# Spreading the retention work over projection slots, using weight slabs one by one over eight PSUM banks, threading transposes between matmuls, and reordering the first loads

## The chip, the cores and the metric

The kernel runs on one Trainium2 chip, as the same program on all 8 cores (two dies, cores 0 to 3 and 4 to 7); each core computes one batch element. The time is the device time of the slowest core in microseconds (us).

In most executions the runs agree within 0.3%; in some, the cores of one die or both show a lower granted TensorE clock and the run is longer. All comparisons below use fast runs. Even in fast runs, some *pairs* of cores (0 and 1, 2 and 3, ...) show a stretch of about 150 us at a clock of 0.81, which costs such a pair some 30 us. I therefore compare stages on a core without such a stretch.

Engine names as the profile has them: PE is TensorE (matmul), DVE is VectorE, ACT is ScalarE, POOL is GpSimd, SP is SyncE (here the issuer of the small DMAs; the big weight slabs are issued from POOL's queue).

## The reference, cut to what matters

One transformer-like layer over 2048 tokens of width 2048, plus 256 context tokens:

```python
h  = modulate(rmsnorm(x, norm1_g), sh1, sc1)        # shift, scale, gate from silu(c) @ w_mod
p  = h @ w_in                                       # q, k, v, g_ret, u, vs, two merge gates
ret = bidirectional_retention(rope(q), rope(k), v, lg_f, lg_b, s_f, s_b)  # 8 heads of 256
ret = per_head_rmsnorm(ret) * silu(g_ret)
y_sg = spatial_gating(gelu(u), gelu(vs), ...)       # layernorm(vs), 128x128 mixing of positions
x  = x + gt1 * ((sig(gr) * (ret @ w_ret_o) + sig(gs) * (y_sg @ w_sg_o)) @ w_out)
h2 = modulate(rmsnorm(x, norm2_g), sh2, sc2)
x  = x + gt2 * ((silu(a) * b) @ w_ffn_out)          # a, b = split(h2 @ w_ffn_in), width 5632
return rmsnorm(x, final_norm_g)
```

The kernel goes through it in this order: modulation columns (`wm` slabs); head by head keys and values (`wk`, `wv`), then queries and output gates (`wq`, `wg`) with the retention itself in between; then for each half of the tokens the gate values (`wvs`), the gate inputs (`wu`), the two merged branches (`wgr`, `wgs`), the output projection (`wo`), and the FFN in and out (`wfi`, `wfo`, twice, since the hidden width is split in two).

## The kernel before

All work is issued by a small framework that records reads and writes and adds semaphore waits. Each engine runs its instructions in program order. Weights come through a stream of four slab buffers: `WS.next` takes the next loaded slab, `WS.done` gives its buffer to the next load. The parts that matter here:

```python
# start: everything small first, then the weight stream
dist = ...; F.dma("sp", dist[:], distd); ...; F.dma("sp", wsf[:], sgw...)
WS.pump()
load_x(xkeys[:6])
... # decay tables of all heads on VectorE and ScalarE, each stored to DRAM (two buffers)
... # wsT: transposes of the small mixing weights
norm_x(0, xkeys[0:4])                       # norm of token block 0: ScalarE squares, VectorE rest
for s in range(16):
    mod_cols(s, bank(s % 4))                # 32 tiny matmuls, VectorE adds the bias and frees the bank
    if s == 11:
        F.wait("sp", WS.tickets[12]); load_x(xkeys[6:10])
# ...
# retention pieces are threaded between projections: a "slot" is one projection unit
RV = Rr([2, 3]); RO = Rr([4, 5]); RA = Rr([6, 7])          # rings of PSUM banks
def q_unit(ib, wq):
    ...
    for dst, tt_ in ((qf, tf), (qb, tb)):                    # decayed queries, both on POOL
        F.tt("pool", dst, q, tt_, ALU.mult)
    at(n + 2, lambda: scores(2 * ib + 1)); at(n + 2, lambda: scores(2 * ib))
    at(n + 3, lambda: outp(2 * ib + 1));   at(n + 4, lambda: outp(2 * ib))
for ib in (3, 2, 1, 0):
    at(n, lambda ib=ib: b_step(2 * ib + 1)); at(n + 2, lambda ib=ib: b_step(2 * ib))
    at(n + 3, lambda ib=ib: mod_cols(16 + 4 * h + 3 - ib, bank(RA.get())))
    q_unit(ib, wq); g_unit(2 * ib + 1, wg); g_unit(2 * ib, wg)
# ...
# FFN out (the wo and wvs stages are alike): all slabs of a column block are held together
for nb in range(4):
    w = [WS.next("wfo") for _ in range(3)]
    gt = gate_tab(1, nb)
    for c in range(8):                                       # 8 row chunks of 128 tokens
        ps = bank(RUU.get())                                 # ring of six banks
        for k in range(22):
            F.mm(ps, chunk(aT, k, c), w[k // 8][0][:, k % 8, :], k == 0, k == 21, ...)
        ... # VectorE: ps * gate, added to the residual rows; at the end the final norm and store
    WS.done(*w)
```

## Time and profile before

5296.42, 5298.40, 5305.88 and 5301.71 us. The profiled run took 5349.7 us, since cores 0 and 1 had two stretches at 0.81; core 5 had none.

To find where the time is, I read the start of each matmul from the timeline and sum what the matmuls take back to back: 0.216 us for 512 columns, 0.109 for 256, 0.0555 for 128, 0.0266 for 2. That sum is about 4600 us for the 26,671 matmuls. The rest, before, is waits over 0.5 us (544 us, of which 39 are the time after the last matmul), matmuls at a slow clock (119 us), and the time before the first matmul (34 us).

The view of waits says what ended PE's idle time. Its columns: what PE was about to do, what it waited for with the source line, then microseconds in total, times, and the longest. Kernel before, core 5:

```profile
PE ps L278 <- DVE modp_47 L302: 53.3, 9, 15.4
PE ps L281 <- DVE wsb_330 L311: 42.1, 1, 42.1
...
PE ps L278 <- DMA wfo_25729<-w_fo: 30.0, 4, 8.2
PE ps L278 <- DMA wfo_26233<-w_fo: 28.0, 4, 7.2
PE ps L281 <- DVE xb_1835 L299: 27.1, 8, 10.8
...
PE ps L278 <- DVE Sb_6065 L306: 12.5, 2, 6.4
```

The number after a name is a buffer, so the `Sb` wait comes back for every head under another number, two waits of about 6 us each; with one of about 5 us on `modp` and the slow matmuls after them it makes up the loss of the query phase.

The table of stretches gives busy time per engine and the granted clock (PEclk). Here the query phase of head 0, one FFN-out stage, and one FFN-in stage, kernel before, core 5:

```profile
core 5: us, PE busy (x) PEld busy (x) DVE busy (x) ACT busy (x) POOL busy (x), PEclk, DMA share, GB/s
331.00:429.70 98.70, 81.13 (x676) 57.30 (x674) 54.83 (x120) 20.43 (x49) 30.77 (x23) 0.90 0.34 62
2777.70:2960.30 182.60, 159.04 (x706) 69.58 (x705) 43.58 (x63) 0.00 (x0) 5.30 (x10) 0.93 0.28 57
4775.60:5079.50 303.90, 303.90 (x1409) 137.75 (x1408) 30.94 (x45) 26.27 (x44) 12.68 (x24) 1.00 0.46 87
```

FFN in is full and at full clock: 303.9 us for 1408 matmuls of 0.216 us. The other two lose time twice, once waiting and once at a lower clock after the wait (0.90 and 0.93).

### The profile page before, as it was taken

To read this page: it belongs to the slowest core of one execution; us is meant where nothing else is said; L and a number is where in the kernel's file an instruction comes from. 1 tells how busy PE (TensorE), PEld (TensorE's weight loads), DVE (VectorE), ACT (ScalarE), POOL (GpSimd) and SP (SyncE) were. 2 spreads that over 40 slices of the span, in tenths; PEclk is the share of its full clock that TensorE was granted. 3 is DMA by queue.
4 is the path that set the end of the run, shared out by engine and by line. 5 is a ranking of instruction groups with operands and counts; after the bars stand their busy time and mean duration, and the time that the engine had idled before them with its cause. 6 is when DMAs were issued, how large, how long until landed. Compare 5 with 4: busy or idle time off the path is not lost.

```text
span 5348.6 us, 67778 instructions; the slowest of 8 cores (5283.3 to 5348.6 us)
## 1 busy us (share of the span) xinstructions
PE 4791.8 (90%) x26671; PEld 2508.4 (47%) x26671; DVE 1471.5 (28%) x2964; ACT 798.8 (15%) x1529; POOL 550.5 (10%) x588
## 2 busy tenths in 40 slices
PE   0479889988998999989998999889999999989996
PEld 0356666666664444434443444344444444434442
DVE  1244444444343421013012111244100220121014
ACT  2232221222121210003000000112000120000010
POOL 0022222222221001110000000000111000000000
PEclk9889987998798999999999999999999999989998
DMA  8733342334234444453433444354444534335433
GB/s 179 186 67 65 52 76 36 64 52 76 38 58 69 86 91 76 79 131 67 84 77 61 79 79 105 78 129 78 96 79 78 135 67 76 65 69 87 78 69 99
DMA packets 94344, 443.13 MB, mean 83 GB/s; under 512 B 9456, under 2 KB 35408, under 8 KB 49232
## 3 DMA queue, kind: packets, MB, share of 16 engines
q0 software_dynamic: 47232, 339.76, 36.8%
q1 hardware_dynamic: 46800, 99.03, 5.7%
q8 instruction: 217, 3.56, 0.3%
q14 instruction: 95, 0.78, 0.1%
HBM read 744.93 MB, written 33.57 MB: 146 GB/s over the span
## 4 chain that ended last, share of the span: by engine, by line
PE 79%; DVE 8%; DMA 7%; issue 3%; ACT 2%; DVEq 0%; SPq 0%; another core or an unknown queue 0%; POOL 0%; ACTq 0%; POOLq 0%
PE ps L278 78%; PE ps L281 1%; DMA rc_1202<-k_rope_c 1%; DMA wm_86<-w_mod 1%; DMA wfo_26230<-w_fo 1%; DMA gtab_35088<-gate_d 1%; DMA gtab_22908<-gate_d 1%; DMA wfo_26233<-w_fo 0%; DVEq L181 0%; DMA wfo_25990<-w_fo 0%; DMA stA_58<-norm_g 0%; DMA wfo_25903<-w_fo 0%; DMA wfo_26701<-w_fo 0%; DMA wv_961<-w_qkvg 0%; DMA wvs_17843<-w_vs 0%
## 5 line engine op out<-in xcount | busy, mean ns | idle before, releaser
L278 PE MATMUL ps<-sT_54,wm_86 128*128 128x2 bf16 x640 | 19.5, 164 | 67.8 <-DVE modp_47 L302 14.9
L278 PE MATMUL ps<-sT_54,wm_88 128*128 128x2 bf16 x640 | 19.3, 164 | 53.9 <-DMA wm_88<-w_mod 10.8
L278 PEld LDWEIGHTS ps<-sT_54,wm_86 128*128 128x128 bf16 x640 | 19.0, 101 | 70.3 <-issue 70.0
L259 POOL DMA_DIRECT2D wfi_23549<-w_fi x22 | 11.7, 530 | 345.3 <-PE ps L278 345.3
L259 POOL DMA_DIRECT2D wfi_23918<-w_fi x22 | 11.6, 528 | 331.9 <-PE ps L278 331.9
L278 PEld LDWEIGHTS ps<-sT_54,wm_88 128*128 128x128 bf16 x640 | 18.7, 100 | 56.3 <-issue 56.1
L259 POOL DMA_DIRECT2D wfi_23914<-w_fi x22 | 11.7, 530 | 309.9 <-PE ps L278 309.9
L302 DVE TENSOR_TENSOR modp_47<-ps,fmB_49 128x4 f32<-128x4 f32 x48 | 7.7, 160 | 119.5 <-PE ps L278 119.2
L281 PE MATMUL ps<-identb_44,xb_1835 128*128 128x128 bf16 x128 | 14.0, 287 | 29.2 <-DVE xb_1835 L299 27.1
L281 PE MATMUL ps<-identb_44,wsb_330 128*128 128x128 bf16 x8 | 1.0, 305 | 43.2 <-DVE wsb_330 L311 43.2
L292 ACT ACTIVATE sa_26969<-ps 128x512 f32<-128x512 f32 x7 | 4.2, 597 | 231.0 <-PE ps L278 231.0
L292 ACT ACTIVATE sa_39115<-ps 128x512 f32<-128x512 f32 x7 | 4.2, 598 | 226.6 <-PE ps L278 226.6
L259 POOL DMA_DIRECT2D wfi_23553<-w_fi x22 | 11.7, 531 | 225.3 <-PE ps L278 225.3
L281 PE MATMUL ps<-identf_43,stA_58 96*128 96x96 f32 x1 | 0.4, 391 | 33.0 <-DMA identf_43<-k_ident 33.0
L281 PEld LDWEIGHTS ps<-identb_44,xb_1835 128*128 128x128 bf16 x128 | 12.0, 131 | 31.2 <-issue 31.1
L281 PE MATMUL ps<-identb_44,xb_35878 128*128 128x128 bf16 x128 | 13.8, 274 | 12.7 <-ACT h_28837 L292 4.6
L259 POOL DMA_DIRECT2D wfo_26233<-w_fo x8 | 4.3, 534 | 194.7 <-PE ps L278 194.7
L259 POOL DMA_DIRECT2D wfo_25729<-w_fo x8 | 4.3, 533 | 191.3 <-PE ps L278 191.3
L278 PE MATMUL ps<-h_28837,wfi_23914 128*128 128x512 bf16 x88 | 23.5, 391 | 0.0
L278 PE MATMUL ps<-h_28838,wfi_23914 128*128 128x512 bf16 x88 | 23.5, 391 | 0.0
L278 PE MATMUL ps<-h_1597,wfi_23914 128*128 128x512 bf16 x88 | 23.5, 390 | 0.0
L278 PE MATMUL ps<-h_1596,wfi_23914 128*128 128x512 bf16 x88 | 23.5, 390 | 0.0
(4815 smaller groups left out, 11113.7 us busy)
## 6 DMA issues: line engine op xcount, KB each, us to landing
wfi_23549<-w_fi POOLq DMA_DIRECT2D x22, 1024.0 KB, 8.6
wfi_23553<-w_fi POOLq DMA_DIRECT2D x22, 1024.0 KB, 8.6
wfi_23914<-w_fi POOLq DMA_DIRECT2D x22, 1024.0 KB, 8.7
wfi_23918<-w_fi POOLq DMA_DIRECT2D x22, 1024.0 KB, 8.7
wm_86<-w_mod POOLq DMA_DIRECT2D x20, 1024.0 KB, 10.0
wm_88<-w_mod POOLq DMA_DIRECT2D x20, 1024.0 KB, 12.8
wgs_19532<-w_gsg POOLq DMA_DIRECT2D x16, 1024.0 KB, 8.4
wgr_19674<-w_gret POOLq DMA_DIRECT2D x16, 1024.0 KB, 12.8
```

Of the source, the lines that this page charges most:

```text
L259: E["e"].dma_start(out=out, in_=in_).then_inc(self.sems[k], 16)
L278: return self.op("pe", lambda e: e.matmul(out, lhsT=lhsT, rhs=rhs, start=start, stop=stop), [lhsT, rhs], [out], inc)
L281: return self.op("pe", lambda e: e.transpose(out=out, in_=in_, identity=ident), [in_, ident], [out], inc)
L292: return self.op("act", lambda e: e.activation(**kw), reads, [out] + ([accum] if accum is not None else []))
L302: return self.op(en, lambda e: e.tensor_tensor(out=out, in0=a, in1=b, op=op), [a, b], [out])
```

## The change

No matmul is added or removed. The intent is to take the waits away:

- **Retention:** the rings of two banks become one of four, the pieces get slots of their own, one decay multiply goes from POOL to DVE, and three of the four modulation slabs of a head move.
- **Slabs one by one:** wvs, wo and wfo use each slab as it comes, with all 8 row chunks accumulating in 8 banks, and give it back at once. Exceptions: the first column block of wvs in the first half, the last two of wo, and the last of the second FFN pass in each half of the tokens still hold their slabs together.
- **Transposes** of the second norm go between the matmuls of wo and FFN in.
- **First loads:** identity and small vectors, then the weight stream, then x; the context, the mixing weights and later rope parts come later.
- **An allocator** that prefers memory freed long ago, and tiles in smaller pieces.

```diff
-            F.dma("sp", stA[16 * i:16 * (i + 1), :], src)
-        F.dma("sp", identf[:], identd)
+            tk = F.dma("sp", stA[16 * i:16 * (i + 1), :], src)
+        F.wait("pool", tk)
+        WS.pump()
 # ... (x tiles of block 0, then dist, idx, jdx, wsf)
+        norm_x(0, xkeys[0:4])
         ab = F.tile("ab", ...)                    # decay vector, then the loop over the tables
-        tg = [F.tile("tg", [128, 1024]) for _ in range(2)]
+        tg = [F.tile("tg", [128, 1024]) for _ in range(4)]
 # ...
         for s in range(16):
             mod_cols(s, bank(s % 4))
-            if s == 11:
-                F.wait("sp", WS.tickets[12])
-                load_x(xkeys[6:10])
+        F.wait("sp", WS.tickets[16])
+        load_x(xkeys[6:10])
+        load_rope(1)
+        load_x(xkeys[4:6])
 # ...
-        RV = Rr([2, 3]); RO = Rr([4, 5]); RA = Rr([6, 7])
+        RV = Rr([2, 3]); RA = Rr([4, 5, 6, 7])
 # ... in q_unit and the loop around it
+                decay("pool", qb, tb)
+                at(n, lambda: b_step(2 * ib + 1))
+                at(n + 1, lambda: b_step(2 * ib))
+                at(n + 1, lambda: decay("dve", qf, tf))
                 at(n + 2, lambda: scores(2 * ib + 1))
-                at(n + 2, lambda: scores(2 * ib))
+                at(n + 3, lambda: scores(2 * ib))
                 at(n + 3, lambda: outp(2 * ib + 1))
-                at(n + 4, lambda: outp(2 * ib))
+                at(n + 5, lambda: outp(2 * ib))
 # ... between wvs and wu: the 16 loads of the retention output come here now, ahead of the bias
+            ret = [Multi(F, "ret", NK, 512, BF16, 4) for _ in range(2)]
+            ...     F.dma("sp", part[:, :, j * 256:(j + 1) * 256], ret_d[bb, :, k0:k1, :], ...)
             rsb = F.tile("rsb", [128, H, 128]); bsb = F.tile("bsb", [128, H, 128])
             F.dma("sp", bsb[:].rearrange("p g i -> p (g i)"), sgb.partition_broadcast(128))
 # ... FFN out (wvs and wo alike, but for the exceptions named above)
-                    w = [WS.next("wfo") for _ in range(3)]
-                    for c in range(8): ...
+                        for k0, k1 in FO_PARTS:                     # (0, 6), (6, 14), (14, 22)
+                            w = WS.next("wfo")
+                            for c in range(8):
+                                gemm(bank(c), ..., k0, k1, 22)
+                                if k1 == 22:
+                                    residual(bank(c), 1, nb, c, g == 1)
+                            WS.done(w)
```

## The prediction

> Numbers are core 5's (span 5298.8 us, like the unprofiled 5298.4).
>
> **What bounds the kernel.** TensorE. The timeline spaces back-to-back matmuls 0.216 us apart (512 columns), 0.109 (256), 0.0555 (128), 0.0266 (2). Summed over all 26,671 this is 4602 us. The rest is 544 us in gaps over 0.5 us, 119 of slow matmuls, and 34 before the first one. The waits view names the gaps.
> - Start: projections begin at 186 us. DVE wsb 42, DMA identf 34, DVE modp 15, wm slabs 60.
> - Head 0, keys and values: 144.6 us against 80.3 of matmuls.
> - Query phase: 98 us against 75.2 in every head. Two 6 us waits on DVE Sb (PE wants one of two PSUM banks that a late DVE has not read), one of 5 on modp, then cold matmuls.
> - FFN output (wfo): 7-9 us at nearly every change of column block, since three slabs of four slots are held together; with cold matmuls 28-30 us in each of four stages.
> - Output projection: 29 and 24 us lost (gate table behind the x3 loads, transposes). Gate-value slabs (wvs): 10 and 17.
> - Tail: DVE takes 8.34 us per row chunk, PE 4.75; DVE ends about 33 us after PE.
>
> The cold matmuls: the Trainium skill ("TensorE: Matmul & The Clock Gate", Part 1) says an idle window of about 3.4 us halves the PE clock. The trace agrees: after a 9.3 us wfo wait, core 1's next 8 matmuls took 3.57 us (446 ns each). So a removed wait gains twice.
>
> **What the change does.** No matmul is added or removed.
> - PSUM rotation 2+2 becomes one of 4 and the work gets separate slots; one decay multiply moves from POOL (2.13 us) to DVE (about 1.2). DVE then has about 16 us per query block, plus what POOL blocks it (its tiny ops stretch from 0.16 to 2 us while POOL runs), against PE's 18.8. So I leave 5 us of loss per head: 98 to about 80, gain 140.
> - Start: small loads before weights, wsT later. 16 slabs at 6.3 us (measured spacing) remain the floor. Projections at about 150: gain 36.
> - Head 0: smaller rope loads, but the norm chain (ACT 8.4 us, then DVE) still stands before each block: gain 30.
> - wfo slab by slab over 8 banks: each slab is used for 10-14 us and loads in 6-8, so the waits vanish: gain 110. wvs: gain 22.
> - Output projection: x3 and gates earlier, transposes between matmuls: gain 48; first FFN slabs: 14.
> - Tail: gain 2.
>
> Sum about 400: 4898. Denser PE may draw more 13/16 clock: cores 0 and 1 had two stretches at 0.81 of about 150 us, costing some 30 us each. The skill's same part expects it under all-core load; the trace shows all-core FFN stretches at 1.00, so I add only 20.
>
> **Predicted: 4920 us, 4840 to 5010.** Faster by over 2%: 0.97; within 2%: 0.02; slower: 0.01.
>
> **Shown right or wrong by:** query phase at 77-83 us per head with no DVE Sb waits; wfo stages within 4 us of 152 (but for the tail); no gtab wait; first wk matmul at 140-160 us; tail still DVE, about 33 us.
>
> **What would make it wrong.** DVE becomes the limit of the query phase (it stays near 90 us: +80 in total). 13/16 clock on more cores (+30 each). The new allocator reuses memory early, so loads wait on readers. Head 0 stays DMA bound.

One figure in it is misread: 9.3 us is the slab's piece in the chain view. PE itself stood idle for 8.3 us before those 8 matmuls.

## The result, and the profile after

Fast runs after: 5042.58 and 5049.56 us. The ratio of the fast runs to those of before is 0.952, 95% interval 0.9497 to 0.9543. (A ratio here is the mean time of one kernel's fast runs over that of the other's of the same rounds.) The change is clearly faster, but the prediction of 4920 us and its range, 4840 to 5010, were wrong: a third of the expected gain is missing. The waits view of the kernel after, core 1:

```profile
PE ps L279 <- DMA wm<-w_mod: 64.4, 10, 11.2
PE ps L279 <- DVE modp L303: 55.0, 1, 55.0
PE ps L279 <- DVE tg L303: 28.6, 5, 6.9
PE ps L279 <- DVE sTt L303: 26.5, 16, 2.2
PE ps L282 <- DVE wsb L312: 26.2, 1, 26.2
PE ps L279 <- DVE tm L307: 21.3, 7, 14.8
...
PE ps L279 <- ACT vsf L293: 13.9, 2, 7.0
```

The waits on `wfo` and on `Sb` are gone. New are one wait of 55 us on `modp`, three of the five on `tg` (there were two before, of 14.2 and 8.9 us, in wo), one of 14.8 us on `tm`, and two of 7.0 us on `vsf`. The stretches that answer those shown of before (query phase of head 0, an FFN-out stage, an FFN-in stage), core 1:

```profile
core 1: us, PE busy (x) PEld busy (x) DVE busy (x) ACT busy (x) POOL busy (x), PEclk, DMA share, GB/s
336.70:415.00 78.30, 74.62 (x667) 54.79 (x665) 43.81 (x108) 19.52 (x49) 21.48 (x18) 1.00 0.50 89
2640.00:2792.00 152.00, 152.00 (x706) 68.88 (x704) 40.04 (x58) 0.60 (x1) 6.33 (x12) 1.00 0.43 80
4560.00:4860.00 300.00, 300.00 (x1391) 136.03 (x1390) 28.88 (x42) 25.08 (x42) 11.22 (x22) 1.00 0.45 82
```

Both changed stages now hold the full clock. Stage by stage (from the first matmul with a stage's weights to the first of the next; microseconds; "predicted" is the term in the prediction's sum):

| stage | before, core 5 | after, core 1 | change | predicted |
|---|---|---|---|---|
| start to first wk matmul | 186.4 | 174.0 | -12.4 | -36 |
| head 0, keys and values | 144.6 | 162.7 | +18.1 | -30 |
| queries and gates, 8 heads | 782.4 | 639.9 | -142.5 | -140 |
| keys and values, heads 1 to 7 | 512.6 | 519.9 | +7.3 | 0 |
| gate values wvs, 2 halves | 252.2 | 269.5 | +17.3 | -22 |
| gate inputs wu, 2 halves | 244.7 | 256.6 | +11.9 | 0 |
| merged branches, 2 halves | 888.1 | 894.6 | +6.5 | 0 |
| output projection wo, 2 halves | 281.1 | 248.7 | -32.4 | -48 |
| FFN in, 4 stages | 1241.7 | 1226.8 | -14.9 | -14 |
| FFN out, 4 stages, with the tail | 765.0 | 648.3 | -116.7 | -112 |
| sum | 5298.8 | 5041.0 | -257.8 | -402 |

The big terms, queries and FFN out, came as predicted. The missing 144 us are spread over the start and head 0 (72), wvs (39), wu (12), wo (16) and small ones. Three views show new waits. The start, PE's timeline (start, duration, instruction, and in brackets the idle time before it with what ended it):

```profile
49.41 0.99 PE L279 MATMUL ps<-sT,wm 128*128 128x2 bf16 x32 [8.21 <-DMA wm<-w_mod]
105.40 3.55 PE L279 MATMUL ps<-sT,wm 128*128 128x2 bf16 x128 [55.01 <-DVE modp L303]
120.19 0.99 PE L279 MATMUL ps<-sT,wm 128*128 128x2 bf16 x32 [11.24 <-DMA wm<-w_mod]
```

PE used four slabs by 50 us, then waited for DVE to read a bank of modulation columns. In DVE's program order this addition stands behind the norm of block 0 and the eight decay tables. PE could not give its slabs back, so the stream of weights stood still; the other slabs came afterwards 5.0 to 8.0 us apart (6.7 on average), and the first wk matmul stood behind them at 174.

This order on DVE is not new. In the kernel before, too, tables and norm stood ahead of the additions, and DVE made the first ones at nearly the same time (kernel before, core 5):

```profile
102.14 0.95 DVE L302 TENSOR_TENSOR modp_47<-ps,fmB_49 128x4 f32<-128x4 f32 x4
```

And the kernel after, core 1, where DVE first waits 38 us for the squares of the norm:

```profile
71.99 0.17 DVE L300 TENSOR_SCALAR rs_m<-ssq 128x4 f32<-128x4 f32 x1 [38.34 <-ACT xb L293]
105.10 0.95 DVE L303 TENSOR_TENSOR modp<-ps,fmB 128x4 f32<-128x4 f32 x4
```

Before, PE spent that time waiting 42.1 us on `wsb` and then 15.4 on `modp`; the change took `wsb` out of the way and left one wait of 55.0. The x tiles of block 0, which ACT squares, are now asked for at 15 to 18 us instead of 38 to 40, but behind the weight stream: the last of them took 52.0 us to land and came at 69.7 us (before 19.8 us, at 60.0).

The first wu stage, SP's issues of DMAs, and DVE's own waits in 1650 to 1680 us:

```profile
1631.91 35.29 SPq L260 DMA_DIRECT2D ret<-ret_d  x16
1667.29 0.89 SPq L260 DMA_DIRECT2D bsb<-sg_b  x1
```

```profile
DVE addt L307 <- DMA bsb<-sg_b: 36.4, 1, 36.4
```

The bias load of a few rows stands behind 16 loads that take 35 us to issue, DVE waits for it, and PE waits 14.8 us for DVE (`tm`).

The second wvs stage, which follows the last FFN-out block of the first half, PE:

```profile
3251.98 5.34 PE L279 MATMUL ps<-wvs,h 128*128 128x512 bf16 x24
3263.41 3.57 PE L279 MATMUL ps<-wvs,h 128*128 128x512 bf16 x8 [6.08 <-DVE tg L303]
3272.11 3.17 PE L279 MATMUL ps<-wvs,h 128*128 128x512 bf16 x8 [5.13 <-DVE tg L303]
3281.10 29.26 PE L279 MATMUL ps<-wvs,h 128*128 128x512 bf16 x126 [5.81 <-DVE tg L303]
```

DVE still works on the final norm, 8.62 us per row chunk against PE's 4.75, and wvs now wants all eight banks in its first pass, where before it took a ring of four. These three waits are 17.0 us. A fourth, of 7.0 us on `vsf`, ends both wvs stages: the row sums of the mixing weights use a bank of the pair 6 and 7, which wvs now fills too, and wait for ACT to read it. The 8 matmuls after the first wait took 3.57 us, 446 ns each, so they ran at half speed too.

### The profile page after: what moved, and what is told of

Same layout as the page of the kernel before. It is cut to its first block, busy times and chain, and to the rows that moved or that the text cites. A ratio compares the mean times of both kernels' runs of the same rounds, so it can differ in the third digit from the quotient of the medians.

```text
span 5041.4 us, 68033 instructions; the slowest of 8 cores (5014.0 to 5041.4 us)
## 1 busy us (share of the span) xinstructions
PE 4655.7 (92%) x26671; PEld 2460.9 (49%) x26671; DVE 1438.4 (29%) x3076; ACT 803.0 (16%) x1577; POOL 483.3 (10%) x556
## 4 chain that ended last, share of the span: by engine, by line
PE 82%; DVE 7%; DMA 5%; issue 3%; ACT 2%; SPq 1%; DVEq 0%; another core or an unknown queue 0%; ACTq 0%; POOL 0%; POOLq 0%
PE ps L279 81%; DMA xt<-x 1%; DVE rs_t L303 1%; PE ps L282 1%; SPq L260 1%; DVE rs_m L300 1%; DMA wm<-w_mod 1%; DMA x_35252<-x 1%; DVE rst L307 1%; DMA x_22924<-x 0%; DMA wk<-w_qkvg 0%; ACT r L293 0%; ACT xb L293 0%; DVE xb L300 0%; DVEq L182 0%
## 5 line engine op out<-in xcount | busy, mean ns | idle before, releaser
L279 PE MATMUL ps<-h,wfi 128*128 128x512 bf16 x5632 | 1221.5, 379 | 0.0
L279 PEld LDWEIGHTS ps<-h,wfi 128*128 128x128 bf16 x5632 | 549.9, 98 | 657.1
L279 PE MATMUL ps<-wfo,aT 128*128 128x512 bf16 x2816 | 608.4, 379 | 0.0
L279 PEld LDWEIGHTS ps<-wfo,aT 128*128 128x128 bf16 x2816 | 275.5, 98 | 332.3
L279 PE MATMUL ps<-wv,h 128*128 128x256 bf16 x2304 | 264.2, 273 | 0.0
L279 PE MATMUL ps<-h,wq 128*128 128x512 bf16 x1024 | 240.4, 391 | 0.0
L279 PE MATMUL ps<-h,wu 128*128 128x512 bf16 x1024 | 235.4, 386 | 0.0
L279 PE MATMUL ps<-sgT,wgs 128*128 128x512 bf16 x1024 | 234.8, 383 | 0.0
L279 PE MATMUL ps<-wg,h 128*128 128x256 bf16 x2048 | 234.0, 273 | 0.0
L279 PE MATMUL ps<-h,wgs 128*128 128x512 bf16 x1024 | 231.5, 379 | 0.0
```

Of the source, the lines that this page charges most:

```text
L279: return self.op("pe", lambda e: e.matmul(out, lhsT=lhsT, rhs=rhs, start=start, stop=stop), [lhsT, rhs], [out], inc)
```

## The experiments

Each experiment edits the kernel after. All results were correct. I judge them by stage times on an undisturbed core, since the total of a single look shifts by up to 40 us with the 0.81 stretches.

### 1. The modulation columns ahead of the norm

```diff
-        norm_x(0, xkeys[0:4])
+        for s in range(8):
+            mod_cols(s, bank(s % 4))
         ab = F.tile("ab", ...)          # decay vector and tables
 # ...
-        for s in range(16):
+        for s in range(8, 12):
             mod_cols(s, bank(s % 4))
+        norm_x(0, xkeys[0:4])
+        for s in range(12, 16): ...
```

> The changed kernel with one edit: the modulation columns 0 to 11 are placed before the norm of token block 0 (the decay tables after column 7), so that VectorE's additions (modp) no longer stand behind work that waits for the x tiles. Theory (program order on VectorE): the 55 us wait of PE on DVE modp disappears, the 16 wm slabs stream without a pause, the first wk matmul moves from 174 us to 135-150 us, and the whole run is 25-40 us shorter. Rival (the start is bound by the DMA engines alone): the wait only changes its name to DMA wm, and the first wk matmul stays at 165 us or later.

Measured: fast run 5060.16 us (two pairs of cores at 0.97 mean clock). On core 0 (5006.4 us, clock 0.981) the first wk came at 165.2, head 0's keys and values took 156.4, and the first query matmul came at 321.6 (172.2, 163.4 and 335.6 on core 0 of the kernel after). The wait on `modp` shrank from 55 to 30.8 us, and another took its place on DVE and SP:

```profile
DVE tg L300 <- DMA tab_d<-tg: 38.2, 1, 38.2
```

```profile
98.17 43.79 SPq L260 DMA_DIRECT2D tab_d<-tg  x8
```

So program order on DVE is a cause, and the second thing in the way is the table loop: with four buffers for eight tables it waits until a table has been stored, and the stores share the transfer engines with the slabs. The gain was about half of the expected one, and 165.2 us alone would also fit the rival (165 or later); experiment 9 decides.

### 2. The x tiles of block 1 earlier

```diff
-        F.wait("sp", WS.tickets[16])
+        F.wait("sp", WS.tickets[12])
```

> The changed kernel with one edit: the x tiles of block 1 are requested when weight slab 12 has landed, as in the kernel before, and not when slab 16 (wk) has landed. Theory (the request comes too late): the wait of PE before the transposes of block 1 (26.2 us, on DVE wsb, which stands behind the norm of block 1) shrinks by 15 us or more, wk lands up to 12 us later, and the query phase of head 0 starts 10-25 us earlier than 336.7 us. Rival (DMA engines are simply full): what the tiles gain, wk loses, and the query phase of head 0 starts within 5 us of 336.7.

Measured: 5048.48 us; core 1: first wk 178.8 (4.8 later), head 0's keys and values 159.1 (3.6 shorter), first query at 337.9 against 336.7. What head 0 wins the start loses: the transfers are shared. The Trainium skill says so in "DMA: Bandwidth & Descriptors", section "Issuing engines are not separate DMA queues": transfers started by different engines run on the same 16 DMA engines and interleave. This run agrees: the wk slab of POOL's queue took 33.3 us to land beside SP's x tiles, 23.0 without them.

### 3. The bias load ahead of the ret loads

```diff
+            rsb = F.tile("rsb", ...); bsb = F.tile("bsb", ...)
+            F.dma("sp", bsb[:]..., sgb.partition_broadcast(128))
             ret = [Multi(F, "ret", NK, 512, BF16, 4) for _ in range(2)]
             ... # 16 loads
-            rsb = F.tile("rsb", ...); bsb = F.tile("bsb", ...)
-            F.dma("sp", bsb[:]..., sgb.partition_broadcast(128))
```

> The changed kernel with one edit: the small bias load (bsb) is issued before the 16 loads of the retention result (ret) instead of after them. Theory (the bias waits its turn in the SP queue, which spends 35 us issuing ret): the 14.8 us wait on DVE tm in the first u stage goes, that stage falls from 136.5 to 119-123 us, the second stays near 120. Rival (VectorE is late because of the layer-norm pieces and the later start of the mixing): the stage stays above 132 us.

Measured: 5047.32 us fast (two pairs of cores with a stretch at 0.81; core 1 without one took 5013.2). First wu stage 119.5 us on core 1, 119.3 to 119.9 on the seven other cores (the second stage 118.8 to 119.9, but 142.4 on cores 6 and 7, where their stretch at 0.81 fell on it); without the edit the eight cores of the kernel after spread from 125.0 to 136.5. The theory holds. The spread also says that this wait depends on what else the loads meet, so it can change by ten microseconds when something unrelated is edited (see 8).

### 4. The final norm by four row chunks

```diff
                             residual(ps, 1, nb, c, True)
-                            ssq = F.tile("ssq", [128, 1]); ...     # one root per chunk
+                            if c % 4 < 3:
+                                continue
+                            ssq = F.tile("ssq", [128, 4]); ...     # one root for four chunks
```

> The changed kernel with one edit: the final norm is done for four row chunks at a time, so the chain of 13 small VectorE operations runs 2 times and not 8 times in each half. Theory (VectorE is the limit of the last column block, 8.6 us per chunk against 4.75 on PE, and its backlog is what the gate-value stage of the second half waits for through the 8 PSUM banks): the second gate-value stage falls from 140.9 to 112-122 us with no wait on DVE tg above 3 us, and the last FFN output stage from 192.6 to 170-178 us. Rival (the second gate-value stage waits for its weight slabs or for memory that is freed late): that stage stays above 132 us, and only the end of the kernel gains.

Measured: 5025.6 us fast. The last stage went from 192.6 to 178.1 us as expected, but the second wvs stage stayed at 143.2 (140.9 in the kernel after). The waits on `tg` were gone there, and another had come. ACT's timeline of core 1:

```profile
3304.59 2.07 ACT L293 ACTIVATE vsf<-ps 128x512 f32<-128x512 f32 x4 [34.63 <-DMA out<-x]
```

ACT, which evacuates wvs's banks, waited 34.6 us for a *store* of the output: the buffer it writes was an output row whose store was still under way, since 32 stores were now issued in one go (59 us on SP). The expected gain of this stage had turned into a new wait. By its numbers this is the rival's outcome (the stage above 132 us, memory freed late, a gain at the end alone); but without the edit the named waits were those on `tg`, so either thing alone holds this stage at about 140.

### 5. The retention: two rings of two banks again

```diff
-        RV = Rr([2, 3]); RA = Rr([4, 5, 6, 7])
+        RV = Rr([2, 3]); RO = Rr([4, 5]); RA = Rr([6, 7])
 # in outp:
-                ps = bank(RA.get())
+                ps = bank(RO.get())
```

> The after kernel with one part undone: the retention pieces again rotate over two pairs of PSUM banks (outputs on 4 and 5, all else on 6 and 7) instead of one ring of four; the new slots stay. Stage times on an undisturbed core. Theory A (the ring of four is what made the query phase faster, since a piece no longer waits for the reader of the piece before last): the query phase goes from 80 us per head back to 90 to 98, and waits on Sb or the modulation columns return. Theory B (the spreading over slots is what did it): it stays at 79 to 83 us. Rest of the kernel unchanged within 3 us per stage. In total 5040 under B, 5120 to 5180 under A.

Measured: 5053.27 us fast. The query phase took 80.6 to 82.0 us per head on core 5, 81.2 on average, against 80.0 in the kernel after. `Sb` waits came back, but small ones:

```profile
PE ps L279 <- DVE Sb L307: 26.8, 8, 3.7
```

The ring of four is worth about 1 us per head.

### 6. The retention: the old slots, with the ring of four

```diff
-                at(n, lambda: b_step(2 * ib + 1))
-                at(n + 1, lambda: b_step(2 * ib))
-                at(n + 1, lambda: decay("dve", qf, tf))
                 at(n + 2, lambda: scores(2 * ib + 1))
-                at(n + 3, lambda: scores(2 * ib))
+                at(n + 2, lambda: scores(2 * ib))
                 at(n + 3, lambda: outp(2 * ib + 1))
-                at(n + 5, lambda: outp(2 * ib))
+                at(n + 4, lambda: outp(2 * ib))
 # and both decays on POOL, backward steps and modulation columns in their slots of before
```

> The opposite half: the ring of four banks stays, but the retention pieces go back to the slots of before (backward step and its read in the slots of before, both score pieces in one slot, the decayed query back on POOL, modulation columns in the fourth slot of every block). Theory A (the ring does it): query phase 79 to 84 us per head. Theory B (the slots do it): 90 to 98 us with the waits on Sb and the modulation columns back. If both are needed, this and the run with two pairs of banks both lose 5 us or more per head.

Measured: 5216.78 us in its fast run (cores 2 and 3 at a clock of 0.95). On core 5 the query phase took 94.1 to 94.6 us per head. The waits of PE there:

```profile
PE ps L279 <- DVE r L307: 74.7, 16, 5.0
PE ps L279 <- DVE modp L303: 38.0, 8, 5.0
```

Both runs together: of the 18 us that the query phase lost per head, some 14 (94.3 against 80.0) come from the placing of the pieces and of one multiply, which were not tried apart, 1 from the ring; the other 2 belong to neither alone. Theory B holds, though the waits came back on `r` and `modp` and not on `Sb`. With the old slots PE waits three times per head for nearly 5 us, and the Trainium skill ("TensorE: Matmul & The Clock Gate", Part 1, table of the two states) has the clock halve after an idle window of about 3.4 us; here the mean clock was 0.93 in this run's query phase of head 0, 0.98 with the two rings and the new slots, whose longest wait was 3.7 us.

### 7. FFN out with three slabs held together

```diff
-                        for k0, k1 in FO_PARTS:
-                            w = WS.next("wfo")
-                            for c in range(8): ...
-                            WS.done(w)
+                        w = [WS.next("wfo") for _ in range(3)]
+                        for c in range(8):
+                            ps = bank(RG.get())
+                            for i, (k0, k1) in enumerate(FO_PARTS): ...
+                        WS.done(*w)
```

> The FFN output again takes three slabs together and goes through the row chunks once, over the ring of six banks; all else as in the kernel after. Theory (holding three of four slab buffers starves the next column block): the three inner FFN output stages go from 151.9 back to 175 to 183 us, with some 3 to 5 waits of 6 to 9 us on a wfo slab each, and the matmuls just after such a wait take about 0.43 us each instead of 0.216. Rival (the old waits came from elsewhere, such as stores or other loads in the queue, and slab order is not it): within 5 us of 151.9. Total 5100 to 5170 against 5040 to 5060.

Measured: 5158.53 us fast. The inner FFN-out stages took 175.1, 194.9 and 177.5 us on core 5 (151.9 each after; the middle one, counted to the first wvs matmul, ends with a wait of 19.9 us on `tg`, which in the kernel after falls inside wvs). The third of these stages, PE:

```profile
4459.59 3.57 PE L279 MATMUL ps<-wfo,aT 128*128 128x512 bf16 x8 [3.83 <-DMA wfo<-w_fo]
4464.45 38.60 PE L279 MATMUL ps<-wfo,aT 128*128 128x512 bf16 x168 [1.29 <-DMA wfo<-w_fo]
4508.99 3.57 PE L279 MATMUL ps<-wfo,aT 128*128 128x512 bf16 x8 [5.93 <-DMA wfo<-w_fo]
```

The theory holds: waits at each change of column block, each followed by 8 matmuls at a slow clock (446 ns each; 425 in one of the three cases). Of the 25.6 us of this stage 17.6 are such waits, the rest is the slow clock after them and smaller gaps: here a wait cost about half as much again as its length.

### 8. The residual rows by column blocks

```diff
             for c in range(2, 8):
-                load_x3(c)                            # all four column blocks of a chunk
+                x3.append([F.tile("x3", [128, 512]) for _ in range(4)])
+            for nb in range(4):
+                for c in range(2, 8):
+                    F.dma("sp", x3[c][nb][:], x[...])  # one column block of all chunks
+                if nb < 2:
+                    gts[0, nb + 1] = gate_tab(0, nb + 1)
```

> The residual rows for the output projection are loaded column block by column block (the first 512 columns of all chunks first) rather than chunk by chunk, with the gate rows between. Theory (the 4 to 7 us waits left in the output projection are VectorE waiting for the rows of late chunks, which shows at TensorE as a wait on the gated product): the output projection goes from 125.6 and 123.1 us to 115 to 119 in both halves, ideal 114. Rival (it is the transfers sharing the DMA engines with the weight slabs, whatever their order): it stays within 3 us. Total changes by 6 to 16 us under the theory.

Measured: 5046.12 us. The output projection took 116.9 and 116.6 us on all eight cores (118.6 to 126.3 in the kernel after, over cores and halves), so the theory holds, and the two halves together save 47.6 us against before (281.1 to 233.5), the 48 of the prediction. The order is not the only thing that can take this loss away: without the edit one half reached 116.6 to 117.0 in other runs (the first half on seven cores of experiment 3, the second on five of experiment 5), and why is open. With the edit both halves are there on every core, here and in experiments 10 to 14. Yet the total did not move, since the wu stages took 139.4 us each on core 1 (136.5 and 120.1 before the edit; 121.6 to 139.4 over cores and halves), with 39.6 us of waits on `tm`: in the second half, too, the ret loads now took 34.7 us to issue, and the bias load stood behind them. The gain was lost again to the wait of experiment 3, where both mends are needed together.

### 9. The tables after the transposes of block 0

The decay vector first, columns 0 to 7, norm of block 0, columns 8 to 15, and the loop over the tables (two buffers) only after `trans_x(0, ...)`.

> The kernel after, with the start put in the order of need on VectorE: decay vector first, modulation columns 0 to 7, the norm of block 0, columns 8 to 15, and the loop over the eight decay tables (which in the first experiment made VectorE wait 38 us for table stores) only after the transposes of block 0. Theory (VectorE's program order stops the stream of slabs): no wait on modp over 15 us, first wk matmul at 138 to 152 us (174 after, 165 in the first experiment), queries of head 0 starting at 300 to 322 (337 after). Rival (the transfers alone set it): first wk at 160 or later. A third outcome, first wk early but queries of head 0 still at 330 or later, would say that head 0 has its own limit, the x tiles and the norm chain.

Measured: 5065.24 us in the fast run (mean clocks 0.972 to 0.976). On core 1 the first wk came at 143.7 us and PE's waits on `modp` were gone, so the first half of the theory holds, and the first wk is earlier than the prediction's 150. But the first query came at 351.2, later than in either kernel, so nothing was won. The third outcome came with it: head 0's keys and values took 207.5 us, because DVE now waited for the table stores (45.2 us in five waits) while PE waited behind it 47.9 us for the rotated keys. The wait had moved into head 0.

### 10. All mends together

Late tables as in 9, bias first, residual rows by column blocks, the final norm by four chunks in the second half and by two in the first, and the sums of the mixing weights after the first wu slab (this takes the wait on `vsf`, 7.0 us in each half, away).

> All the mends together: the late tables as above, the bias load ahead of the ret loads, the residual rows by column blocks, the final norm by four row chunks in the second half and by two in the first, and the row sums for the gate values after the first wu slab instead of ahead of it. If the parts add up: first wk at about 145 (gain 25 to 30), both wu stages at 118 to 120 (gain 17), wo 117 in both halves (gain 15), last FFN output stage 178 (gain 14), second wvs stage at 120 to 132 (gain 9 to 20), 6 us each of the wait on vsf gone: 4945 to 4975 us against 5042 to 5050 for the kernel after and 5296 to 5306 before, a ratio of 0.933 to 0.94. If they do not add up (one wait hidden behind another): 4985 to 5020.

Measured: fast runs 4971.55 to 4986.26 us (five), ratio to before in the same rounds 0.9284, interval 0.9236 to 0.9332. (The three fast runs of before in these rounds took 5336 to 5387 us, so this ratio flatters; against the 5300 us of the first rounds it would be 0.938 to 0.941.) On core 1 the wvs stages took 118.7 and 115.1, wu 118.4 and 118.2, wo 116.7 and 116.6, the last stage 175.7. Those parts add up. Grouping by two and moving the row sums were not run apart, so the mending of wvs is shown for the two together. Head 0's keys and values took 206.4 us, so the gain of the start (first wk at 141.9) is given back. DVE's waits in 100 to 350 us:

```profile
DVE tg L300 <- DMA tab_d<-tg: 44.6, 5, 37.6
```

### 11. The same with the next block's norm ahead of the projections

```diff
+                if h == 0 and 0 < ib < 3:
+                    norm_x(ib + 1, xkeys[6 + 4 * ib:10 + 4 * ib])
                 k_unit(ib); v_unit(2 * ib); v_unit(2 * ib + 1)
```

> As the run of all mends, with the norm of the next block of head 0 issued ahead of this block's projections from block 1 on. Theory (in head 0 PE waits for the norm behind the evacuations on ScalarE and VectorE): keys and values of head 0 in 140 to 150 us instead of 155 to 163, the wait on xb of 15 us gone, total 8 to 15 us under the run before. Rival (the x tiles land late, whatever the order): the same within 4 us, or worse as the evacuations now wait behind the norm.

Measured: 4975.14 to 4982.84 us (three fast runs), no better than the run before in the same rounds, though head 0 took 196.8 us on core 1, 9.6 less. In its profiled run four cores had a clock of 0.978 or 0.979, against 0.981 and up in the run before; but core 1, at 0.981, gave the gain back as well, 5.7 us in the queries and 8.3 in wvs. The stage agrees with the theory, the total with the rival; by itself this is inconclusive.

### 12. The tables spread over head 0

Tables of heads 0 and 1 after the transposes of block 0, the others two by two after the value units, each in a buffer of its own.

> The run of all mends, but with the tables of heads 0 and 1 after the transposes of block 0 and the other six two by two after the value units of head 0's blocks, each in a buffer of its own. Theory (VectorE waited for a table store, and everything of head 0 behind it): no wait of PE on kT above 5 us, first wk still at 140 to 145, first query of head 0 at 295 to 318 (348 in the run of all mends, 337 in the kernel after), total 4930 to 4950. Rival (the x tiles land late, the wait merely had another name): first query at 335 or later, total within 8 us of 4973.

Measured: 4973.37 to 4978.19 us (four fast runs); first query at 349.9 us. The named wait was gone (PE's on kT was 0.8 us) and nothing was won, which are the rival's numbers; DVE's view in 140 to 350 us shows why:

```profile
DVE kb L300 <- DMA tab_d<-tg: 31.2, 1, 31.2
```

The decayed keys were written into the memory of a table that had been *freed* in the program, but whose store had not finished. Two stores took 21.3 and 16.4 us to land, the other six 2.6 to 3.0: those two were issued behind six tiles of 1 MB (four of x, two of the context) that were still under way.

### 13. The same with the norm ahead

> The run before with the norm of the next block of head 0 ahead of this block's projections from block 1 on. If the norm chain (8 us of squares on ScalarE, 3.5 us of root, 4.9 us of scaling, one after the other) stands before each block's transposes, keys and values of head 0 shorten by 8 to 25 us and the wait of 15 us on xb goes; if the x tiles land too late for it, nothing changes.

Measured: 4957.66 and 4961.17 us fast. Head 0's keys and values took 187.8 us (207.7 without), and the transposes' waits on `xb`, 28.6 us, are gone: the norm chain was worth 20 us. The pending store remained (32.3 us on `kb`).

### 14. The tables among the slabs

Each table is made and stored after one of the columns 8 to 15, ahead of the x tiles, in eight buffers that live until block 0 is transposed; the norm ahead as in 13.

```diff
         for s in range(8, 16):
             mod_cols(s, bank(s % 4))
+            make_tab(s - 8)
```

> As the last run (all mends, norm ahead), but each table is made and stored after one of the modulation columns 8 to 15, in eight buffers that stay until block 0 is transposed, so the stores come ahead of the x tiles. Theory (a pending table store held VectorE): no wait of VectorE on a table store above 5 us; first wk at 145 to 156 (4 MB of stores now share with the slabs); PE's wait on the small weights 20 to 35 us instead of 53; first query at 305 to 320 instead of 331; total 4930 to 4950. Rival (the x tiles of block 1 are what is awaited): first query at 328 to 342, total 4950 to 4970.

Measured: five fast runs, 4933.48 to 4951.30 us, ratio to before in the same rounds 0.9289, interval 0.9273 to 0.9305 (on this chip before took 5313 to 5320 us). First wk at 146.8, first query at 311.4 us. DVE waited for no table store any more, though the stores took longer than before to land (21.1 to 50.6 us, beside the slabs): what helped is that nothing needed their buffers meanwhile. It also answers the rival: the x tiles of block 1 landed later than in 13 (at 181 to 191 us instead of 165 to 177), and the first query still came 20 us earlier. What is left of head 0 in PE's view, core 1, 146 to 312 us:

```profile
PE ps L282 <- DVE wsb L312: 40.5, 1, 40.5
PE ps L282 <- POOL kT L303: 8.1, 2, 7.1
```

The wait on `wsb` (expected at 20 to 35) is now the norm of block 1, behind its x tiles. The transfer engines were busy at 80% and more in all 40 slices of 140 to 190 us, at 255 GB/s on average, so I take the rest of head 0 to be bound by transfers; no run took those transfers away, so this is argued and not shown. This kernel beats the two of the prediction: 0.9289 of before, where the change reached 0.952; the intervals do not touch. They were not run side by side.

## Why the prediction was wrong

**Right:** the bound (PE waits, and slow matmuls after them); the query phase, 98 to 80 us per head (predicted "98 to about 80, gain 140", measured -142.5); FFN out ("the waits vanish", predicted gain 110 and 2 for the tail, measured 116.7, with 151.9 us per inner stage); FFN in (14 against 14.9). The claim that DVE still ends the tail held, 36.7 us after PE (33 expected). The loss of 5 us left per query phase was a guess that came out close (80.0 against 75.2 of matmuls); most of it is waits on `r` and `sTt`, about 4 us per head. For the queries the prediction named the ring and the slots as one; experiments 5 and 6 give the slots some 14 of the 18 us and the ring about 1.

**Wrong, by term:**

1. *"Start: ... Projections at about 150: gain 36"*, got 12.4. I took the slab spacing of 6.3 us as the only floor, with the wait on `wsb` gone, and did not follow DVE's program order, in which the norm of block 0 and the table loop precede the additions that free the banks, as they did before. The first addition came at 105.1 us (102.1 before), so the removed wait came back as 55 us on `modp`; the x tiles, now behind the weight stream, let the norm start only at 72 us. The Trainium skill has DVE strictly in order ("TensorE: Matmul & The Clock Gate", Part 1, section on the array's architecture, on queue depths); the 55 us wait on `modp` agrees. Experiments 1 and 9 show it for the first wk: 165.2 and 143.7 us with the order changed. Missed: 24 us.
2. *"Head 0: smaller rope loads, ... gain 30"*, got a loss of 18.1. The x tiles of block 1 are asked for only when the 16 slabs are used up; the DMA issues on SP show them at 172.62 us, and PE waits 26.2 us for `wsb` behind their norm. Asking earlier alone does not help (experiment 2), as start and head share the transfers. Missed: 48 us. What pays is the norm ahead of the projections and tables whose pending stores hold nobody (experiments 13 and 14), 20 us each. Start and head 0 were predicted to gain 66 us together and lost 5.7; the best run (14) has its first query at 311.4 us against 331.0 before, a gain of 19.6. So most of this part of the prediction was reached by no run. "Head 0 stays DMA bound" was on the prediction's own list of what would make it wrong; experiments 2 and 14 point that way.
3. *"wvs: gain 22"*, got a loss of 17.3. I costed the removed slab waits only. Taking all eight banks makes wvs wait for the slowest reader of the banks: for DVE in the last FFN block (17.0 us of waits in the second stage, and slow matmuls after them), and at the end of both stages for ACT (13.9 us on `vsf`). The first is not mended by grouping the norm by four, which bunches the stores (experiment 4); with groups of two and the row sums moved, in experiment 10, the stages took 118.7 and 115.1 us. Missed: 39 us.
4. wu was taken as unchanged and lost 11.9 us to the moved ret loads in front of the bias load (experiment 3).
5. *"Output projection: ... gain 48"*, got 32.4. The mechanism was right, its size was not: waits for the gated product, which experiment 8 puts down to the load order of the rows, took a third back. With it mended all 48 came.
6. The 20 us allowed for a lower clock were not needed on core 1, which had no stretch at 0.81: all cores had a clock of 0.979 to 0.980 in the profiled run.

The terms missed by 24, 48, 39, 12 and 16 us; with 14 from small ones and 8 the other way (the queries, FFN in and FFN out) this is the whole 144 us. The common failure: I added up waits that the change removes, and did not ask what else stands ahead of the awaited instruction on its engine or queue. (Buffers freed while a transfer was pending came up only in my own mends, experiments 4 and 12.)

**Left open:** why heads 1 to 7 take 1 us more each (PE waits 2 us on `sTt` there; not tried), and what head 0 would be without its transfers.

## What to carry to other kernels

When a change moves work or takes a wait away, list what else stands ahead of the awaited instruction on its in-order engine: a small addition that frees a PSUM bank can hold the weight stream, and through it everything. A removed wait often turns up under another name (`modp`, then `tab_d`, then `kb`), so follow the time of a whole phase to its end, not the wait that you mended. Freed memory is free only when its last transfer has landed: keep the buffer of a store out of use until then, and do not issue many stores at once before a stage that takes over their buffers.

## What the Trainium skill lacked or had wrong

- "TensorE: Matmul & The Clock Gate", Part 1 ("Seeing it yourself", on the peak-current limiter) says that the clock of a whole die falls to 13/16 once three of its cores run dense matmuls, and stays there while the load lasts. Fast runs show otherwise: while all eight cores ran dense matmuls, core 5 held a clock of 1.00 for 303.9 us, and 0.81 came in stretches of about 150 us in pairs of cores (before: cores 0 and 1 at 0.81 from 780 to 930 us, cores 2 and 3 of the same die at 0.95 then). In the last experiment, cores 2 and 3 had a mean of 0.980 and took 4948.1 and 4950.1 us, the other six, cores 0 and 1 of their die among them, 0.985 or 0.986 and 4925.5 to 4931.7. In slow runs a whole die is lower (0.919 to 0.924 on cores 4 to 7 of the run of 5319.94 us).
- Nothing was wrong with the same page's half clock after an idle window of about 3.4 us: 446 ns per 512-column matmul after such waits, and waits of 17.6 us in a stage lengthened it by 25.6 us (experiment 7).
- "DMA: Bandwidth & Descriptors", section "Issuing engines are not separate DMA queues", says that transfers interleave, but gives no figure there for what this does to the time of a store. Here stores of 512 KB took 2.6 to 3.0 us to land, 21.3 and 16.4 us behind six tiles of 1 MB (experiment 12), and 21.1 to 50.6 us beside the weight slabs (experiment 14).
